# One encoder step on one core: the last down pair's second half behind the first, values and turned v in the large products' banks, gates' rows later, GpSimd's shares back on VectorE

## The chip, the cores and the metric

One core of one Trainium2 chip runs the whole kernel. Its engines are TensorE (PE, with its weight loads shown as PEld), VectorE (DVE), ScalarE (ACT), GpSimd (POOL) and SyncE (SP, which starts transfers). The metric is the time of one execution in microseconds (us), as the median of several; the profile comes from one execution of its own.

## The reference

One step of a hybrid streaming encoder layer for 512 prompt frames of a new stream and 64 frames of a running one, width 1024, feed-forward width 2816:

```python
h = layer_norm(ALPHA * x + 0.5 * swiglu_ffn(x, p['ffn1_w_gu'], p['ffn1_w_down']), p['ln1_g'], p['ln1_b'])
mix, new_state = token_mixer(h, p, conv_prev, ml_state, att_past)
h = layer_norm(ALPHA * h + mix, p['ln2_g'], p['ln2_b'])
h = layer_norm(ALPHA * h + 0.5 * swiglu_ffn(h, p['ffn2_w_gu'], p['ffn2_w_down']), p['ln3_g'], p['ln3_b'])
```

`token_mixer` multiplies `h` by one wide matrix `w_in` (mLSTM q, k, v, o, i, f; attention q, k, v; two gates), runs a chunked mLSTM with 4 heads and a band attention with 16 heads, projects both, gates them and multiplies by `w_out`. The states of the mLSTM, of its convolution and the new keys and values are outputs too.

## The kernel before, in words

**Data.** All 576 frames (512 + 64) lie along the free axis, the features in tiles of 128 partitions. A product is taken in three passes with operands split into a high part and a low part (`wh`, `wl` for weights): `wh` times high, `wh` times low, `wl` times high. Each stage works on two halves of the frames (256 + 320, or 288 + 288), so a row of 128x256, 128x288 or 128x320 in the profile is one pass over one 128-row block and one half. Almost all matmuls go through the helpers `mm` (L135) and `transpose` (L145); ScalarE's through `act` (L149), VectorE's and GpSimd's through `tt` (L152), `stt` (L155) and `ts` (L159).

**Weights.** SyncE loads a raw tile (`wr`), ScalarE casts it to `wh`, and the low part is made in one of three ways, by tables at the top: by VectorE in one operation; by VectorE in two halves of 512 columns (`PIECES`); or, for the chunks of `w_in` in `ADDED`, by a ScalarE copy of `-wh` and a GpSimd transfer that adds the raw tile in memory (`add_lo`). `("in", 48)`, `("in", 40)` and `("in", 32)` are the first three chunks of `w_in` that are used: v, k and q of the first attention head pair.

**PSUM.** There are eight banks, four with the tag "aux" (the default of `bank()`) and four with "mm" (large products). A bank is handed out again when everything that reads it is done.

**Order.** TensorE's instructions stand as the program writes them: a small event queue (`Order`) counts TensorE's time in nanoseconds as it writes matmuls, `later(dt, fn)` puts a piece of work `dt` behind, and `tick()` between matmuls lets due pieces in, along with background generators (`od.bg`: a gap and a generator). The other engines' instructions are put in order by the build's scheduler, which `high_priority` and `issue_after` steer.

**Stages that the change touches, by time in the profile.**
- *Last down pair of the first feed-forward (about 360 to 400).* The down product is taken in pairs of output tiles with seven products (`seven`, a Strassen-like scheme) into the banks X and Z (mm) and Y; `ln.take` lets VectorE add a bank to the residual tile `s`. For the last pair (6, 7) some parts are plain products (`plain`). The layer norm's first half can begin when the parts that go to half A are taken: `ln.last` sums squares, then `stats` (1-column matmuls `aux<-onec,s` and a mean), `centre` (eight `s<-s,c`, of which the tiles listed in `CP` go to GpSimd), `spread` and `apply`, and low parts `s<-s,s`. The first product of `w_in` (chunks 48, 40, 32 side by side) follows, and inside it the second half's statistics.
- *Attention (about 580 to 780).* For each pair of heads three large products give v, k and q (two passes of 256 and 320 frames each, into mm banks). q is evicted to `qs` by ScalarE and VectorE, two operations each a pass. `v_tr` turns v on TensorE into an aux bank; scores, softmax, turned probabilities (`pth`, `ptl`; `psh`, `psl` for the 64 sampled frames) and `values` and `values_s` follow from the event queue, in aux banks.
- *Attention's output projection (about 776 to 830).* `os_split` prepares sums of the heads' outputs (`Combos`) for another seven-product scheme: `Combos.begin` gives two of the four sums of tile `i + 1` to GpSimd, `Combos.add` the others to VectorE, `halves` casts the sums into `tx`.
- *mLSTM (about 840 to 1000).* v is turned by `turn5` into aux banks, with `vh` and `vl` read from them.
- *Gates' rows (around 455).* A background generator `gate_rows` takes the logarithms and cumulated sums of i and f on VectorE.
- *Second layer norm (about 1150), and the third in the tail (`turned`),* where one of four output blocks is scaled by ScalarE and GpSimd and three by VectorE.

Of the kernel before, what the change touches and what calls it, by code (L numbers as in the profile page):

```python
# [88 lines left out]
def tile_layer(ctx: ExitStack, tc: tile.TileContext, ins, outs):  # L89
# [87 lines left out]
    PIECES = {("in", 32)}  # L177

    ADDED = {("in", 48), ("in", 40)} | {("in", c + j) for c in (32, 40, 48) for j in range(2, KT)} | {("in", c) for c in (*range(2, 8), *range(10, 32), *range(56, 72))} \
# [6 lines left out]
    CP = (4, 5, 6, 7)  # L186
# [311 lines left out]
    class Norm:  # L498
# [168 lines left out]
        def turned(self, hf, dh, sq):  # L667
# [21 lines left out]
            own = nb - 1, 0  # L689
            for q in range(2):  # L690
                for b in range(nb):
                    z[b, q] = slot(F32)[:, :512]
                    if (b, q) != own:
                        last = stt(z[b, q], pts[b, q], m[:, b:b + 1], self.gb[q], ALU.subtract, ALU.mult)
                    else:
                        with tc.issue_after(last.ins):
                            last = stt(m[:, nb:nb + 1], m[:, b:b + 1], -1.0, rs[:, b:b + 1], ALU.mult, ALU.mult)
                        t = z[own]
                        act(t, pts[own], AF.Identity, scale=rs[:, b:b + 1], bias=m[:, nb:nb + 1])
                        tt(t, t, self.gb[0], ALU.mult, POOL)  # L700
                        tt(t, t, self.gb[2], ALU.add, POOL)
                        SP.dma_start(outs["yt"][b, :, 0:512], t)
            with tc.issue_after(last.ins):
                for (b, q), t in z.items():
                    if (b, q) != own:
                        stt(t, t, rs[:, b:b + 1], self.gb[2 + q], ALU.mult, ALU.add)
                        SP.dma_start(outs["yt"][b, :, q * 512:(q + 1) * 512], t)
# [56 lines left out]
    class Combos:  # L764
# [11 lines left out]
        def begin(self, i):  # L776
            r1, r2 = self.raw[4 + i], self.raw[i]
            a, b = slice(0, HT_), slice(HT_, T)
            u = self.sums[2 * i]
            tt(u[:, a], r1[:, a], r1[:, b], ALU.subtract, POOL)  # L780
            tt(u[:, b], r2[:, b], r1[:, b], ALU.subtract, POOL)

        def add(self, i, begun=False):
# [3 lines left out]
            if not begun:  # L787
                tt(u[:, a], r1[:, a], r1[:, b], ALU.subtract)
            stt(v[:, a], u[:, a], -1.0, r2[:, b], ALU.mult, ALU.subtract)
            if not begun:  # L790
                tt(u[:, b], r2[:, b], r1[:, b], ALU.subtract)
# [319 lines left out]
    def seven(n, j, inner, ln, Y=None):  # L1111
# [40 lines left out]
    def ffn(xs, n, gi, raw, final=None, prev=None):  # L1152
        hh = {}
        with tc.tile_pool(name=nm("hr"), bufs=FT, side="right", reuse_waits="tile") as hr, \
# [82 lines left out]
            with tc.tile_pool(name=nm("h1"), bufs=n1, side="right", reuse_waits="tile") as h1, \  # L1237
# [60 lines left out]
                if n == 1:  # L1298
# [133 lines left out]
    def att_qkv(j):  # L1432
# [119 lines left out]
    def att_core(j, st):  # L1552
# [51 lines left out]
        def values(e):  # L1604
            th, tl = PT[e]
            valued[0] += 1
            po = bank()
# [31 lines left out]
        def values_s(th, tl):  # L1639
            po = bank()  # L1640
# [76 lines left out]
    with tc.tile_pool(name="cx", bufs=1, side="right", reuse_waits="tile") as cx:  # L1717
# [29 lines left out]
        od.bg.append((GR, gate_rows()))  # L1747
# [20 lines left out]
    for j in range(6):  # L1768
# [3 lines left out]
        if j == 3:  # L1772
# [20 lines left out]
            def os_split():  # L1793
# [126 lines left out]
    def turn5(src, sink):  # L1920
# [392 lines left out]
```

## Time and profile before

| | |
|---|---|
| Median of 3 runs | 1563.18 us (1562.06 to 1565.11) |
| The profiled execution | 1561.61 us, its span 1559.9 us |
| TensorE busy | 1535.5 us (98% of the span) |
| VectorE, ScalarE, GpSimd busy | 73%, 57%, 16% |
| TensorE's mean granted clock | 0.995 |

A row of the profile's timeline reads: start, duration, engine, line of the kernel, operation, output tile <- inputs (numbers left out), shape, count, and in brackets the idle time before it and what ended that. A row of waits reads: engine, waiting tile and line, what it waited for, then us in total, number of times, longest. Matmuls are pipelined, so neighbouring ones overlap in the records; their pace is read from their starts.

### The profile page before, as it was taken

Reading aid. Unit: us, or ns where it says so; the run is one execution under the profiler, and the core shown is the slowest. Engines: PE = TensorE matmul, PEld = TensorE weight load, DVE = VectorE, ACT = ScalarE, POOL = GpSimd, SP = SyncE. Lnnn points to the kernel's source line nnn. Section 1 sums busy time; section 2 is a strip of 40 time slices with the busy share of each in tenths; the row PEclk is TensorE's granted clock in tenths of the full one; section 3 lists DMA queues with packets and bytes.
Section 4 is the critical chain, followed back from the end, with each engine's and each line's share of the span. In section 5 each row is a group of like instructions: output and inputs, shape, how many; then the busy total and the mean of one; then the engine's idle time right before and its main releaser. Section 6 shows DMA issues by size and latency. Waiting matters only on the chain.

```text
span 1559.9 us, 29496 instructions
## 1 busy us (share of the span) xinstructions
PE 1535.5 (98%) x11579; PEld 1520.6 (97%) x11579; DVE 1140.2 (73%) x2090; ACT 893.8 (57%) x1683; POOL 246.9 (16%) x451
## 2 busy tenths in 40 slices
PE   9999999999899999999999999999999999999997
PEld 9999999999899999999999999999999999999997
DVE  7877778676788766777586766755676877788755
ACT  7544457334665557777754877753466454557333
POOL 1000001001310015555311212202131000001002
PEclk9999999999899999999999999999999999999999
DMA  9232324534764348686534765642665222226344
GB/s 260 107 109 82 109 82 102 143 100 122 192 159 165 131 134 219 165 209 168 121 136 140 190 145 133 162 148 82 196 151 129 109 82 108 82 74 143 118 117 144
DMA packets 80836, 213.11 MB, mean 137 GB/s; under 512 B 9145, under 2 KB 21049, under 8 KB 80697
## 3 DMA queue, kind: packets, MB, share of 16 engines
q1 hardware_dynamic: 65432, 170.07, 33.1%
q0 software_dynamic: 12096, 35.33, 13.0%
q10 hardware_dynamic: 3168, 5.83, 1.1%
q8 instruction: 91, 1.49, 0.4%
q14 instruction: 49, 0.39, 0.1%
HBM read 174.23 MB, written 21.63 MB: 126 GB/s over the span
## 4 chain that ended last, share of the span: by engine, by line
PE 83%; DVE 6%; ACT 5%; DMA 2%; issue 2%; POOL 2%; DVEq 0%; SPq 0%; POOLq 0%; ACTq 0%
PE mm L135 67%; PE aux L135 14%; PE aux L145 2%; DVE wl L152 1%; DVE s L152 1%; ACT s L149 1%; ACT wh L149 1%; DMA wl<-in_w_in 1%; DMA w<-in_w_gu 1%; ACT sc L149 1%; POOL kh L159 0%; DMA wr<-in_w_dn 0%; DVE s L155 0%; ACT wh L868 0%; DVE sc L1572 0%
## 5 line engine op out<-in xcount | busy, mean ns | idle before, releaser
L135 PE MATMUL mm<-s,wh 128*128 128x288 f32 (+2 forms) x3667 | 753.6, 298 | 1.9 <-DVE st L155 0.9
L135 PEld LDWEIGHTS mm<-s,wh 128*128 128x128 f32 x3667 | 589.9, 189 | 5.7 <-DVE st L155 1.5
L135 PE MATMUL mm<-s,wl 128*128 128x288 f32 (+2 forms) x1806 | 534.5, 296 | 5.6 <-DMA wl<-in_w_in 5.6
L135 PEld LDWEIGHTS mm<-s,wl 128*128 128x128 f32 x1806 | 341.2, 189 | 6.0 <-DMA wl<-in_w_in 6.0
L149 ACT ACTIVATE wh<-wr 128x1024 fp32r<-128x1024 f32 (+2 forms) x133 | 134.2, 1016 | 148.0 <-PE mm L135 86.9
L152 DVE TENSOR_TENSOR wl<-wr,wh 128x1024 fp32r<-128x1024 f32 (+2 forms) x91 | 108.4, 1200 | 52.5 <-ACT wh L149 51.5
L135 PE MATMUL mm<-tx,wh 128*128 128x288 f32 x677 | 140.4, 296 | 0.8 <-DVE tx L152 0.8
L135 PEld LDWEIGHTS mm<-tx,wh 128*128 128x128 f32 x677 | 109.2, 188 | 1.2 <-DVE tx L152 1.0
L152 DVE TENSOR_TENSOR wl<-wt,wh 128x1024 fp32r<-128x1024 f32 x51 | 63.6, 1248 | 55.5 <-ACT wh L868 55.5
L135 PE MATMUL mm<-tx,wl 128*128 128x288 f32 x350 | 103.2, 295 | 0.0
L868 ACT ACTIVATE wh<-wt 128x1024 fp32r<-128x1024 f32 x51 | 54.0, 1059 | 84.2 <-DVE wt L152 84.2
L152 DVE TENSOR_TENSOR wl<-wu,wh 128x1024 fp32r<-128x1024 f32 x63 | 77.1, 1223 | 31.3 <-ACT wh L868 31.3
L868 ACT ACTIVATE wh<-wu 128x1024 fp32r<-128x1024 f32 x63 | 66.7, 1058 | 40.9 <-PE mm L135 35.3
L196 POOL DMA_DIRECT2D s<-s x16 | 13.7, 859 | 469.5 <-DVE hb L152 217.7
L135 PE MATMUL mm<-tx,ah 128*128 128x288 f32 x416 | 85.5, 297 | 0.4 <-ACT c L149 0.2
L149 ACT ACTIVATE h<-h 128x288 f32<-128x288 f32 x78 | 34.0, 436 | 61.0 <-DVE h L152 60.9
L135 PEld LDWEIGHTS mm<-tx,ah 128*128 128x128 f32 x416 | 66.2, 188 | 1.2 <-ACT c L149 0.6
L135 PEld LDWEIGHTS mm<-tx,wl 128*128 128x128 f32 x350 | 65.7, 188 | 0.0
L152 DVE TENSOR_TENSOR ws<-wu 128x1024 f32<-128x1024 f32 (+1 forms) x55 | 64.7, 1176 | 0.0
L152 DVE TENSOR_TENSOR wl<-ws,wh 128x1024 fp32r<-128x1024 f32 x51 | 62.2, 1219 | 3.0 <-ACT wh L868 3.0
L135 PE MATMUL mm<-h,wh 128*128 128x288 f32 (+2 forms) x304 | 62.7, 296 | 0.1
L135 PE MATMUL mm<-tx,al 128*128 128x288 f32 x208 | 61.1, 294 | 0.0
(400 smaller groups left out, 3497.3 us busy)
## 6 DMA issues: line engine op xcount, KB each, us to landing
wu<-in_w_gu SPq DMA_DIRECT2D x78, 512.0 KB, 4.4
wr<-in_w_in SPq DMA_DIRECT2D x48, 512.0 KB, 4.1
wr<-in_w_dn SPq DMA_DIRECT2D x38, 512.0 KB, 3.6
wl<-in_w_in POOLq DMA_DIRECT2D x38, 512.0 KB, 6.7
wu<-in_w_in SPq DMA_DIRECT2D x24, 512.0 KB, 4.6
wr<-in_w_dn SPq DMA_DIRECT2D x20, 384.0 KB, 4.0
s<-s POOLq DMA_DIRECT2D x16, 288.0 KB, 4.8
wu<-in_w_ap SPq DMA_DIRECT2D x8, 512.0 KB, 4.6
```

Source lines behind the costliest of these rows:

```text
L135: PE.matmul(out, lhsT, rhs, start=start, stop=stop, **kw)
L145: PE.transpose(out, in_, idn)
L149: return ACT.activation(out, in_, func, **kw)
L152: return (eng or DVE).tensor_tensor(out, a, b, op=op)
L196: return POOL.dma_start(lo, src, accum_op=ALU.add)
L868: self.last = ACT.activation(hi, src, AF.Copy)
```

## The change

1. `("in", 48)` and `("in", 40)` move from `ADDED` to `PIECES`: their low parts are made by VectorE in halves. In `seven` for pair (6, 7) the two Z products (`q1` with `t1`, `t1` with `b22`) move behind `q0 t3` and `a22 t4`, and the last takes and sums of the first half stand ahead of them (`first`).
2. `CP` becomes (6, 7): GpSimd centres two tiles of eight instead of four, in every layer norm.
3. `values`, `values_s`, `v_tr` (from the third head pair on) and the mLSTM's `turn5` of v take a "mm" bank.
4. `gate_rows` is handed to the background 20000 ns later.
5. `Combos.begin` goes, all four sums of a tile are VectorE's, with a priority for the third and fourth tile; and in the tail VectorE scales all four blocks.

```diff
-    PIECES = {("in", 32)}
-    ADDED = {("in", 48), ("in", 40)} | {("in", c + j) for c in (32, 40, 48) for j in range(2, KT)} | ...
+    PIECES = {("in", 48), ("in", 40), ("in", 32)}
+    ADDED = {("in", c + j) for c in (32, 40, 48) for j in range(2, KT)} | ...
-    CP = (4, 5, 6, 7)
+    CP = (6, 7)
...
-    def seven(n, j, inner, ln, Y=None):
+    def seven(n, j, inner, ln, Y=None, first=False):
         product(X, "t0", "t2", False)
         ln.take(j, B, X, ALU.add)
-        product(Z, "q1", "t1", True)
-        ln.take(j + 1, B, Z, ALU.subtract)
+        if not first:
+            product(Z, "q1", "t1", True)
+            ln.take(j + 1, B, Z, ALU.subtract)
         product(X, "q0", "t3", False, "v")
         ln.take(j + 1, B, X, ALU.subtract)
-        product(Z, "t1", "b22", False, "t")
-        product(X, "a22", "t4", False, "u")
+        if not first:
+            product(Z, "t1", "b22", False, "t")
+        product(X, "a22", "t4", False, None if first else "u")
         ln.take(j + 1, A, X, ALU.subtract)
+        if first:
+            first()
+            product(Z, "q1", "t1", True, "u")
+            ln.take(j + 1, B, Z, ALU.subtract)
+            product(Z, "t1", "b22", False, "t")
...
-                    Y, Z = seven(n, 6, inner, ln, Y)
-                    ln.take(6, A, Y, ALU.add)
-                    ln.last(6, A)
-                    ln.last(7, A)
+                    def first():
+                        ln.take(6, A, Y, ALU.add)
+                        ln.last(6, A)
+                        ln.last(7, A)
+                    _, Z = seven(n, 6, inner, ln, Y, first)
...
         def v_tr():
-                ps = bank()
+                ps = bank("mm" if j > 1 else "aux")
         def values(e):
-            po = bank()
+            po = bank("mm")
         def values_s(th, tl):
-            po = bank()
+            po = bank("mm")
...
-        od.bg.append((GR, gate_rows()))
+        later(20000, lambda: od.bg.append((GR, gate_rows())))
...
                 for i in range(4):
-                    if i == 0:
-                        combos.sums[0] = slot(F32)
-                    if i < 3:
-                        combos.sums[2 * i + 2] = slot(F32)
-                        combos.begin(i + 1)
-                    combos.add(i, i > 0)
-                    halves(i, 1)
+                    combos.sums[2 * i] = slot(F32)
+                    with tc.high_priority(offset=60 if i > 1 else 0):
+                        combos.add(i)
+                        halves(i, 1)
                     yield None
-                    halves(i, 0)
+                    with tc.high_priority(offset=60 if i > 1 else 0):
+                        halves(i, 0)
                     yield None
...
-                    turn5(vf, sink)
+                    turn5(vf, sink, "mm")
```

**TensorE at the last down pair.** Before; X is `mm_607`, Z is `mm_608`, and each group is twelve matmuls, of which the first and last are shown. `wh_604` with `s_456` is `q1 t1`, `wh_609` is `q0 t3`, `wh_601` with `h_503` is `t1 b22`, `wh_604` with `s_454` is `a22 t4`.

```order
L135 MATMUL mm_607_4299<-s_486_3286,wl_602_4245 128x288
L135 MATMUL mm_608_4300<-s_456_3161,wh_604_4277 128x288
...
L135 MATMUL mm_608_4300<-s_488_3291,wl_605_4278 128x288
L135 MATMUL mm_607_4299<-s_456_3161,wh_609_4304 128x288
...
L135 MATMUL mm_607_4299<-s_488_3291,wl_610_4305 128x288
L135 MATMUL mm_608_4300<-h_503_3369,wh_601_4244 128x288
...
L135 MATMUL mm_608_4300<-h_509_3417,wl_602_4245 128x288
L135 MATMUL mm_607_4299<-s_454_3156,wh_604_4277 128x288
```

And now, with the same names:

```order
L135 MATMUL mm_607_4299<-s_486_3286,wl_602_4245 128x288
L135 MATMUL mm_607_4299<-s_456_3161,wh_609_4304 128x288
...
L135 MATMUL mm_607_4299<-s_488_3291,wl_610_4305 128x288
L135 MATMUL mm_607_4299<-s_454_3156,wh_604_4277 128x288
...
L135 MATMUL mm_607_4299<-s_486_3286,wl_605_4278 128x288
L135 MATMUL mm_608_4300<-s_456_3161,wh_604_4277 128x288
...
L135 MATMUL mm_608_4300<-s_488_3291,wl_605_4278 128x288
L135 MATMUL aux_620_4404<-onec_143,s1_430_3034 128x1 x3
```

The three products of X now follow each other directly, with nothing of Z between them, and the first half's statistics come right behind `q1 t1`.

**TensorE at the sampled values of a head pair.** Now; `mm_1221` is the second pass of the query's product, `mm_1253` and `mm_1254` the turned v, `mm_1255` the sampled values.

```order
L135 MATMUL mm_1221_8123<-s_654_4589,wl_1144_7707 128x320
L145 MATMUL aux_1239_8229<-ident_133,sc_1223_8132 128x128
...
L135 MATMUL mm_1249_8252<-s_640_4510,wl_1182_7917 128x256
L145 MATMUL mm_1253_8269<-ident_133,s_1174_7904 128x128
...
L145 MATMUL mm_1254_8276<-ident_133,s_1174_7904 64x128
L135 MATMUL mm_1255_8280<-psh_1230_8181,vc_949_6712 64x64
```

Before, the last three tiles were `aux`. In the built program `mm_1255` lies in the bank of `mm_1221`, fifteen instructions behind its last matmul, and its first matmul waits for VectorE's second `qs` of `mm_1221`; the pair of heads after next has the same.

**VectorE at the attention projection's sums.** Before, from the last operation ahead of the third tile's `tx` (`tx_1580`) to the fourth's (`tx_1586`):

```order
L155 SCALAR_TENSOR_TENSOR o_1455_9369<-o_1455_9369,o_1171_7897 128x288
L152 TENSOR_TENSOR tx_1580_10029<-o_1382_8973,tx_1579_10028 128x576
L152 TENSOR_TENSOR wl_1601_10100<-wu_1540_9841,wh_1600_10099 128x1024
L152 TENSOR_TENSOR tx_1582_10033<-s_1572_9983,tx_1581_10032 128x576
L152 TENSOR_TENSOR ws_1605_10119<-wu_1541_9844 128x512
L152 TENSOR_TENSOR o_1593_10062<-mm_1595_10077,o_1593_10062 128x288
L152 TENSOR_TENSOR tx_1586_10043<-o_1455_9369,tx_1585_10042 128x576
```

And now (the third tile's `tx` is `tx_1579`; the fourth's, `tx_1586`, comes four rows behind these):

```order
L152 TENSOR_TENSOR wl_1601_10102<-wu_1540_9843,wh_1600_10101 128x1024
L152 TENSOR_TENSOR tx_1573_9988<-o_1313_8635,tx_1572_9987 128x576
L152 TENSOR_TENSOR ws_1605_10121<-wu_1541_9846 128x512
L152 TENSOR_TENSOR o_1593_10064<-mm_1595_10079,o_1593_10064 128x288
L152 TENSOR_TENSOR tx_1575_10001<-s_1571_9982,tx_1574_10000 128x576
L152 TENSOR_TENSOR wu_1541_9846<-wu_1541_9846 128x512
L152 TENSOR_TENSOR s_1584_10039<-o_1455_9371 128x288
L152 TENSOR_TENSOR s_1584_10039<-o_1171_7899,o_1455_9371 128x288
L155 SCALAR_TENSOR_TENSOR o_1455_9371<-s_1584_10039,o_1171_7899 128x288
L152 TENSOR_TENSOR tx_1579_10028<-o_1382_8975,tx_1578_10027 128x576
```

`wl_1601` stood behind the third tile's `tx` and stands ahead of it now, with the second tile's `tx`, a take and two weight steps, and the fourth tile's sums have come between.

More of the change, by code (lines that the diff above doesn't have):

```diff
@@ L176, in tile_layer @@
     NH0, NH1 = 1, 6
-    PIECES = {("in", 32)}
-    ADDED = {("in", 48), ("in", 40)} | {("in", c + j) for c in (32, 40, 48) for j in range(2, KT)} | {("in", c) for c in (*range(2, 8), *range(10, 32), *range(56, 72))} \
+    PIECES = {("in", 48), ("in", 40), ("in", 32)}
+    ADDED = {("in", c + j) for c in (32, 40, 48) for j in range(2, KT)} | {("in", c) for c in (*range(2, 8), *range(10, 32), *range(56, 72))} \
         | {("gu2", 1, 1), ("gu2", 2, 0), ("gu2", 2, 1)}
@@ L688, in turned @@
             z = {}
-            own = nb - 1, 0
             for q in range(2):
@@ L692, in turned @@
                     z[b, q] = slot(F32)[:, :512]
[L693 to L702, printed above, removed]
+                    last = stt(z[b, q], pts[b, q], m[:, b:b + 1], self.gb[q], ALU.subtract, ALU.mult)
             with tc.issue_after(last.ins):
                 for (b, q), t in z.items():
-                    if (b, q) != own:
-                        stt(t, t, rs[:, b:b + 1], self.gb[2 + q], ALU.mult, ALU.add)
-                        SP.dma_start(outs["yt"][b, :, q * 512:(q + 1) * 512], t)
+                    stt(t, t, rs[:, b:b + 1], self.gb[2 + q], ALU.mult, ALU.add)
+                    SP.dma_start(outs["yt"][b, :, q * 512:(q + 1) * 512], t)
         def centre(self, hf, bc, power):
@@ L774, in tile, with add @@
             return slot(F32R, self.pool, "tx", bufs=self.nx) if self.n <= self.nx else slot(F32R)
[L776 to L783, printed above, removed]
+        def add(self, i):
             r1, r2 = self.raw[4 + i], self.raw[i]
@@ L1918, in conv_rest, with turn5 @@
         return q, hi, lo
-    def turn5(src, sink):
+    def turn5(src, sink, tag="aux"):
         for b0, nb in ((0, 4), (4, 1)):
             w = P if b0 < 4 else NS
-            ps = bank()
+            ps = bank(tag)
             for b in range(nb):
```

6 lines of the change are left out of this document (2 added, 4 removed).

## Prediction

> **What bounds the kernel now.** I read the page first, its busy times, then TensorE's own waits, then the timeline of each place that the diff touches.
>
> ```profile
> PE 1535.5 (98%) x11579; PEld 1520.6 (97%) x11579; DVE 1140.2 (73%) x2090; ACT 893.8 (57%) x1683; POOL 246.9 (16%) x451
> PE mm L135 <- DMA wl<-in_w_in: 5.6, 2, 3.3
> PE aux L145 <- DVE ptl L152: 0.8, 1, 0.8
> PE mm L135 <- DVE st L155: 0.9, 1, 0.9
> ```
>
> TensorE (PE) is busy for 98% of the span, so only its waits can be won: 24 us of 1559.9, of which the largest group is 5.6 us for two weight transfers. The change adds and removes no matmul; it can gain what these waits (and one stretch of slow clock) cost, and it can make new ones.
>
> **Part 1: the boundary of the first layer norm (the last down pair).**
>
> ```profile
> 372.56 0.42 PE L135 MATMUL mm<-s,wh 128*128 128x288 f32 x2
> 373.20 1.23 DVE L152 TENSOR_TENSOR wl<-wr,wh 128x1024 fp32r<-128x1024 f32 x1 [1.29 <-ACT wh L149]
> 374.34 0.45 DVE L152 TENSOR_TENSOR s<-s,mm 128x288 f32<-128x288 f32 x1
> 374.94 0.50 PE L135 MATMUL mm<-s,wh 128*128 128x288 f32 x2 [0.63 <-DVE s L152]
> 376.81 0.45 DVE L152 TENSOR_TENSOR s<-s,mm 128x288 f32<-128x288 f32 x1 [1.29 <-PE mm L135]
> 381.59 0.80 PE L135 MATMUL aux<-onec,s 128*128 128x1 f32 x6
> 383.41 0.51 PE L135 MATMUL mm<-hb,wh 128*128 128x288 f32 x2
> 396.21 0.39 PE L135 MATMUL mm<-s,wl 128*128 128x256 f32 x1 [2.25 <-DMA wl<-in_w_in]
> 400.19 0.58 PE L135 MATMUL mm<-s,wl 128*128 128x256 f32 x1 [3.35 <-DMA wl<-in_w_in]
> 405.86 0.77 PE L135 MATMUL mm<-s,wh 128*128 128x256 f32 x2
> 384.00:393.00 9.00, 9.00 (x68) 8.89 (x67) 6.57 (x16) 7.88 (x15) 6.06 (x8) 1.00 0.68 170
> 397.00:398.00 1.00, 0.00 (x0) 0.00 (x0) 0.77 (x3) 0.04 (x1) 0.00 (x0) 1.00 1.07 279
> 399.00:400.00 1.00, 0.00 (x0) 0.00 (x0) 0.00 (x0) 0.00 (x0) 0.00 (x0) 0.50 0.95 332
> 405.00:408.00 3.00, 3.00 (x15) 3.00 (x16) 1.58 (x4) 1.81 (x6) 1.51 (x2) 0.50 0.06 25
> 409.05:410.85 1.80, 1.80 (x17) 1.80 (x16) 1.80 (x3) 1.43 (x3) 1.80 (x3) 1.00 0.00 0
> ```
>
> The two waits at 396.21 and 400.19 are for the low parts of two weight tiles that GpSimd adds by DMA. The last five lines are windows (their length, then busy times of PE, its weight loads, VectorE, ScalarE and GpSimd with counts, then granted clock, DMA share, GB/s): during the second wait the clock falls to half, and it stays there until past 408.
>
> Now the new order. At full clock a matmul of 288 columns takes 0.133 us (68 in the 9.00 us of 384 to 393) and one of 256 columns 0.12 (17 touch the 1.80 us of 409.05 to 410.85, two of them begun before). The twelve products of q1 with t1 that begin at 372.56 move behind the statistics of the first half. The next group now needs its bank at 372.56, and VectorE (DVE) takes it at 374.34 + 0.45, since its 1.23 us `wl` stands ahead: the wait grows from 0.63 to 2.4 us. Twelve products end at 376.5; the next take (376.81 + 0.45) makes PE wait again, to 377.3. Then twelve products (378.9), twelve more (380.5), the statistics (381.59 to 383.41 is 1.8 now; to 382.3), 54 products and the spread (389.8), 42 products (395.4), 15 of 256 columns (397.2), the second statistics (1.8; 399.0). With 0.5 us for low parts and sums that DVE delivers just in time I come to 399.5, against 405.86: **6.4 us**. Twelve matmuls behind it ran at half clock, 0.2 us each (15 in 3.00 us), and run at 0.12: 1 more. The four low parts by DVE (some 0.65 us a half, as half of the 1.23 us `wl`) and two more centring operations a half (0.45 each) come in stretches where DVE is busy for 6.57 of 9.00 us (384 to 393); ScalarE loses two casts. From 417 on, the other engines set the pace (two windows and one row):
>
> ```profile
> 417.00:437.00 20.00, 20.00 (x143) 19.84 (x143) 13.50 (x29) 19.79 (x40) 6.77 (x8) 1.00 0.97 219
> 437.00:481.00 44.00, 42.81 (x318) 42.09 (x317) 43.49 (x60) 26.20 (x41) 2.29 (x5) 1.00 0.49 142
> 407.38 2.08 DVE L152 TENSOR_TENSOR s<-s,c 128x288 f32<-128x288 f32 x2
> ```
>
> ScalarE is busy for 19.8 of 20 us, then DVE for 43.5 of 44, so PE keeps only what these two gain. They follow the second statistics, and of DVE's chain behind it the slow centring (407.38: 1.04 us each beside GpSimd, against 0.45) gets shorter. I book **-7.0 us**, from -8.3 (all of it) to -3.5 (DVE delivers late at the second statistics).
>
> At the clock I weigh a rule. The rows: the wait of 2.25 us at 396.21 left the clock at 1.00 (397 to 398), and 3.35 us more, after one short burst, brought 0.50. The Trainium skill ("TensorE: Matmul & The Clock Gate", Part 1) says that the clock falls to half after a whole idle window of some 3.4 us, which runs freely. By that rule alone the new 2.4 us wait keeps the full clock and part 1 stays at -7.0; the burst before the fall here was short, so the rows alone leave a smaller wait possible, and I keep the fall as a rival.
>
> **Part 2: values, sampled values and the turned v in the "mm" banks.** This frees "aux" banks, but a mm bank comes free only when the large product that it held has been read.
>
> ```profile
> 679.37 0.27 PE L135 MATMUL aux<-psh,vc 128*64 128x64 f32 x1
> 678.85 1.05 ACT L149 ACTIVATE wh<-wr 128x1024 fp32r<-128x1024 f32 x1
> 681.02 0.43 ACT L149 ACTIVATE qs<-mm 64x320 fp32r<-64x320 f32 x1
> 681.48 0.49 DVE L155 SCALAR_TENSOR_TENSOR qs<-mm,qs 64x320 fp32r<-64x320 f32 x1 [1.42 <-ACT qs L149]
> 634.12 0.19 PE L135 MATMUL aux<-psh,vc 128*64 128x64 f32 x1
> 634.23 0.68 DVE L152 TENSOR_TENSOR o<-aux,tmp 64x512 f32<-64x512 f32 x1
> 963.90 0.40 PE L135 MATMUL mm<-s,wh 128*128 128x256 f32 x2
> 963.89 0.88 DVE L152 TENSOR_TENSOR vl<-aux,vh 128x512 fp32r<-128x512 f32 x2
> 988.73 0.28 PE L135 MATMUL aux<-vh,W 128*128 128x258 f32 x1
> 989.07 0.37 ACT L149 ACTIVATE hf<-aux 128x258 f32<-128x258 f32 x1
> ```
>
> In the changed program the sampled values of two head pairs get the bank of the query's second pass, and their first matmul waits for DVE's last `qs` of it. At the first place that matmul starts at 679.37 now, and the `qs` ends at 681.48 + 0.49, because ScalarE's share of the work (681.02) stands behind two casts of 1.05 us, the first at 678.85. That order doesn't change, so TensorE will wait about 2.6 us there, and as long two head pairs later, where the same instructions follow each other: 5.2. At 634.12 the same matmul gets the bank of the values that DVE reads until 634.92: 0.8 us more, in spite of the 0.8 us wait on `ptl` (in the list above) that goes just before it. In the mLSTM a product that starts at 963.90 gets the bank of a turned v, whose reader is the first of the two `vl` from 963.89 (about 0.7 of their 0.88 us), and a state product at 988.73 a bank that ScalarE reads until 989.07 + 0.37: 0.7 each. Small waits that go, and later ones that shrink because the other engines have caught up, give back 1.2, an estimate. Sum: **+6.2**, from +3.5 (half of the first two places) to +7.5.
>
> **Part 3: the attention projection's sums.**
>
> ```profile
> 797.34 1.06 DVE L155 SCALAR_TENSOR_TENSOR o<-s,o 128x288 f32<-128x288 f32 x1
> 800.06 1.05 ACT L868 ACTIVATE wh<-wu 128x1024 fp32r<-128x1024 f32 x1
> 804.75 0.45 DVE L152 TENSOR_TENSOR o<-mm,o 128x288 f32<-128x288 f32 x1
> 805.12 0.75 DVE L152 TENSOR_TENSOR tx<-o,tx 128x576 fp32r<-128x576 f32 x1
> 805.78 0.69 DVE L152 TENSOR_TENSOR wu<-wu 128x512 f32<-128x512 f32 x1
> 805.92 0.40 PE L135 MATMUL mm<-tx,wh 128*128 128x288 f32 x1 [0.80 <-DVE tx L152]
> ```
>
> Six GpSimd operations go to DVE, where one of 288 columns takes 0.37 us (804.75 to 805.12): 2.2 us more on an engine that PE already waits for at 805.92. GpSimd's shadow goes with them (1.06 against 0.45 at 797.34, and about as much at two more operations), some 1.8. But DVE's order changes too: the third and fourth `tx` now stand behind a `wl`, a take and steps on the weights. That `wl` waits for the cast at 800.06 + 1.05, which I let begin a microsecond earlier, since the `tx` cast ahead of it on ScalarE moves behind it. Walking DVE from 800 (1.2 for `wl`, 0.66 for a `tx`, 0.37 for a sum, 0.63 for a weight step) the third `tx` ends at 806.0 and the fourth at 808.4, so PE's 805.92 becomes 808.4: **+2.5**, from +1.2 to +3.6.
>
> **Part 4: GpSimd's shares at the second layer norm and in the tail; the gates' rows.**
>
> ```profile
> 1164.52 0.39 PE L135 MATMUL mm<-s,eh 128*128 128x256 f32 x1 [0.76 <-DVE s L152]
> 1551.76 3.79 DVE L155 SCALAR_TENSOR_TENSOR s<-s,rs,s 128x512 f32<-128x512 f32 x3
> ```
>
> With two GpSimd operations instead of four, DVE's low parts run undisturbed there, and the wait of 0.76 us and a smaller one ahead of it go: **-1.0** (0 to -1.1). In the tail three operations take 3.79 us beside GpSimd, and undisturbed ones would need some 0.7 each, 1.7 less; against that stand one more operation on DVE in this row and one ahead of it: **-0.6** (0 to -0.9). The gates' rows: DVE's operations for them stand in the same places as before, and only five TensorE transposes move, so the 0.9 us wait on `st` (in the list above) stays: **0** (-0.9 if it goes).
>
> **Sum.** -7.0 + 6.2 + 2.5 - 1.0 - 0.6 = +0.1. The profiled execution took 1561.61 us (span 1559.9 and 1.7 around it), which becomes 1561.7; the median of the runs shown is 1.57 above the profiled one, so I forecast **1563.3 us**: the gain at the first layer norm is spent on bank waits and sums.
>
> **The rivals.** About 0.2% (3.1 us) is what a measurement of this kernel can tell from no change.
> - *Slower, the clock falls.* The wait of 2.4 us at 372.6 and the next of 0.8 us lie within 5 us; if the gate counts them as idle, PE runs at half clock until it has been busy for a while, as from 400.2 to past 408: some 8.4 us at half, so 4.2 us lost, 1567.5. It decides as soon as the clock in 375 to 385 reads under 1.00. For it: the fall at 398 to 399 came after 1.5 to 2 us of an unbroken wait. Against: 2.25 us did nothing. 10%.
> - *Slower, VectorE late at the second statistics.* The low parts and centring operations queue ahead of the last sums, and part 1 brings 3.5: 1566.8. 12%.
> - *Faster, the boundary pays more.* The gates' rows or the shorter centring relieve DVE in 437 to 481, so the wait on `st` goes (0.9), part 1 gives 8.3 and the sums cost 1.2: 1563.3 - 0.9 - 1.3 - 1.3 = 1559.8. 22%.
> - *Faster, the bank waits don't come* (another bank, or `qs` sooner than now): without the 5.2 us 1558.1. Against it stands the fixed order on ScalarE. 8%.
>
> **How the numbers follow.** My forecast has 48%. The two faster cases make 30% for faster by over 0.2%, the two slower ones 22%; 48% within. The range reaches past the cases on both sides by the unknowns of parts 2 and 3: 1557 to 1568. Forecast alone: 1560 to 1566.
>
> **What would show it.** Right: no wait on `wl<-in_w_in` and clock 1.00 in 395 to 410; a wait of about 2.4 us on `s` near 375; two waits of about 2.6 us on `qs` in the attention stage, which nothing there has now; a `tx` wait near 800 of 2 to 3 us instead of 0.8; the tail half a microsecond shorter. Wrong: no `qs` waits, a half clock near 375, or the second statistics later than 401.

## The result, and the profile after

The changed kernel takes **1568.19 us** (median of 14 runs, 1566.21 to 1573.5) against 1562.43 us (14 runs) for the kernel before on the same chips: a ratio of **1.0046, 95% interval 1.0035 to 1.0056**. It is slower by about 0.5%, where 1563.3 and no change had been forecast, and the end of the range (1568.0) is just missed. The profiled execution took 1567.9 us, its span 1566.2: 6.3 more than the profiled execution before.

Three views of the changed kernel. Its busy times, then TensorE's waits (us in total, times, longest), first lines of the list:

```profile
PE 1536.7 (98%) x11579; PEld 1522.5 (97%) x11579; DVE 1143.5 (73%) x2111; ACT 893.1 (57%) x1682; POOL 228.7 (15%) x431
```

```profile
PE mm L135 <- DVE qs L155: 5.0, 2, 2.5
PE mm L135 <- DVE s L152: 2.8, 3, 2.1
PE mm L135 <- DVE tx L152: 2.1, 2, 1.3
PE mm L145 <- DVE qs L155: 1.8, 1, 1.8
PE mm L135 <- ACT vf L149: 1.8, 1, 1.8
...
PE mm L135 <- DVE st L155: 0.9, 1, 0.9
```

The 5.6 us for the two weight transfers are gone, as predicted. In their place stand the waits that the prediction named, at nearly its sizes (two on `qs` of 2.5, one on `s` of 2.1, `tx` of 1.3 and less), the unmoved 0.9 on `st`, and two that it did not have: 1.8 us on `vf`, and 1.8 on `qs` at a turned v (L145). The timeline shows where they are; of a row with a count, the time is that of its first instruction:

```profile
375.43 0.52 PE L135 MATMUL mm<-s,wh 128*128 128x288 f32 x2 [2.09 <-DVE s L152]
414.01 0.56 PE L135 MATMUL mm<-s,wh 128*128 128x320 f32 x2 [1.84 <-ACT vf L149]
680.27 0.22 PE L135 MATMUL mm<-psh,vc 128*64 128x64 f32 x1 [2.50 <-DVE qs L155]
728.87 0.22 PE L135 MATMUL mm<-psh,vc 128*64 128x64 f32 x1 [2.50 <-DVE qs L155]
810.80 0.40 PE L135 MATMUL mm<-tx,wh 128*128 128x288 f32 x1 [1.27 <-DVE tx L152]
813.11 0.61 PE L135 MATMUL mm<-tx,wh 128*128 128x288 f32 x1 [0.83 <-DVE tx L152]
```

The waits alone do not make the time. The windows below (length, busy times of PE, its weight loads, DVE, ScalarE, GpSimd with counts, granted clock, DMA share, GB/s) are cut, but for 395 to 410, on the grid of 3.41 us on which the trace's record of the clock changes. They show, for four of these places, the 3.41 us that hold the wait, or most of it, and the time behind:

```profile
372.40:375.81 3.41, 1.32 (x11) 1.12 (x10) 2.06 (x4) 1.39 (x2) 0.00 (x0) 1.00 0.29 96
375.81:382.64 6.83, 6.28 (x26) 5.94 (x26) 1.87 (x3) 0.84 (x1) 0.00 (x0) 0.50 0.46 134
395.00:410.00 15.00, 15.00 (x119) 14.63 (x119) 13.88 (x32) 9.54 (x24) 7.44 (x9) 1.00 0.72 259
676.18:679.59 3.41, 1.59 (x14) 1.32 (x12) 1.92 (x4) 3.35 (x6) 3.00 (x6) 1.00 0.84 201
679.59:683.00 3.41, 2.73 (x32) 2.76 (x33) 1.73 (x4) 1.79 (x6) 2.83 (x8) 1.00 0.62 168
727.38:730.79 3.41, 1.92 (x26) 1.95 (x27) 1.38 (x3) 2.17 (x7) 2.07 (x6) 1.00 0.78 211
730.79:734.20 3.41, 3.41 (x18) 3.41 (x17) 0.94 (x3) 0.79 (x2) 2.26 (x6) 0.50 0.56 91
809.30:812.71 3.41, 1.17 (x5) 0.48 (x4) 3.41 (x8) 1.59 (x3) 0.00 (x0) 1.00 0.28 113
812.71:816.12 3.41, 3.01 (x12) 3.01 (x13) 2.35 (x4) 1.53 (x3) 0.00 (x0) 0.50 0.49 118
```

Behind three of the new waits TensorE runs at **half clock**, for 6.83, 3.41 and 3.41 us; behind the one at 680 it does not. In 395 to 410, where the clock was at half before, it is 1.00 now. Following each matmul through both traces (the start of the same instruction after, less its start before) gives where the 6.3 us come from: +0.6 by 36 us (in the traces of this study that stretch is 0.0 to 2.1 us longer than in the kernel before's), -3.3 over the first layer norm, +7.5 at the bank waits, +1.3 for the half clock at 731, +2.1 at the `tx` waits, +1.3 for the half clock at 813, -1.0 at the second layer norm and -1.5 in the tail: +7.0, of which steps of 0.3 us and less in between take back 0.7.

The runs differ more than before, and with their clock: the eight with a mean granted clock of 0.993 to 0.995 took 1566.2 to 1568.4 us, the six with 0.990 to 0.992 took 1570.4 to 1573.5.

### The profile page after: what moved, and what is told of

It reads as the page before. It is cut to its first block, busy times and chain, and to the rows that moved or that the text cites. A ratio compares the mean times of both kernels' runs of the same rounds, so it can differ in the third digit from the quotient of the medians.

```text
span 1566.2 us, 29485 instructions
## 1 busy us (share of the span) xinstructions
PE 1536.7 (98%) x11579; PEld 1522.5 (97%) x11579; DVE 1143.5 (73%) x2111; ACT 893.1 (57%) x1682; POOL 228.7 (15%) x431
## 3 DMA queue, kind: packets, MB, share of 16 engines
q8 instruction: 91, 1.49, 0.4%
## 4 chain that ended last, share of the span: by engine, by line
PE 89%; DVE 4%; ACT 4%; POOL 1%; issue 1%; DMA 0%; ACTq 0%; DVEq 0%; POOLq 0%; SPq 0%
PE mm L135 74%; PE aux L135 13%; PE aux L145 1%; DVE wl L152 1%; DVE s L152 1%; ACT wh L149 1%; ACT sc L149 1%; POOL kh L159 1%; DMA wr<-in_w_dn 0%; ACT L149 0%; DVE s L155 0%; DVE sc L1562 0%; ACT s L149 0%; ACT wl L149 0%; PE mm L145 0%
```

## The experiments

Theory: each wait costs its length, and besides, it may halve the clock: the granted clock is set once in every 3.41 us, on a grid that runs freely, and falls when TensorE was idle for too much of one such stretch. So the same wait halves the clock in one execution and not in the next. Rival: the parts cost their waits, as predicted, and the excess is in the parts themselves. Times are medians; the kernel before had 1562.3 to 1562.4 in all three groups of runs.

**e1, the boundary alone.** `PIECES`, `ADDED`, `seven` and the last pair as changed:

```diff
-    PIECES = {("in", 32)}
+    PIECES = {("in", 48), ("in", 40), ("in", 32)}
...
+                    _, Z = seven(n, 6, inner, ln, Y, first)
```

> The kernel before with the first part alone (last down pair's second-half products behind the first half's, low parts of the two weight tiles by VectorE). Theory: the wait of 2.2 us that this order puts near 373 leaves TensorE less than about half busy over one 3.4 us stretch, so the granted clock falls to half for 3.4 to 6.8 us around 376 to 383 in this profile and in most runs, and a new wait of about 1.8 us on vf near 412 takes back what TensorE has won over ScalarE: about 3 us below the kernel before (1559.5), with runs of lower mean clock longer. Rival (the step as predicted): the clock stays at 1.00 there and all of 7 us is kept: 1555.5.

Measured: **1557.86**, ratio 0.9967 (0.9955 to 0.9979). The six runs: 1554.92, 1554.99 and 1556.8 with clocks of 0.998, 0.999 and 0.997; 1558.92, 1560.25 and 1560.83 with 0.994, 0.995 and 0.994. The profiled one is of the first kind. Its windows, on the grid that its own last fall (in the tail) fixes, and the wait on `vf`:

```profile
370.69:374.10 3.41, 2.31 (x17) 2.02 (x16) 2.18 (x4) 1.39 (x2) 0.00 (x0) 1.00 0.65 202
374.10:377.51 3.41, 2.05 (x13) 1.84 (x14) 1.49 (x4) 0.80 (x1) 0.00 (x0) 1.00 0.52 154
377.51:384.00 6.49, 6.49 (x50) 6.38 (x50) 5.04 (x10) 2.02 (x5) 0.81 (x1) 1.00 0.22 64
```

```profile
374.92 0.51 PE L135 MATMUL mm<-s,wh 128*128 128x288 f32 x2 [1.91 <-DVE s L152]
410.48 0.56 PE L135 MATMUL mm<-s,wh 128*128 128x320 f32 x2 [0.65 <-ACT vf L149]
```

The same wait is there, but a border of the grid cuts it: 1.10 us of idle time in one stretch and 1.36 in the next (which also holds a second, short wait), and the clock stays at 1.00. So both expectations were half right: the boundary is worth the predicted 7 us in the two shortest runs (1562.4 - 1555.0 = 7.4), and 1.6 to 3.5 in the three with the lower clock. Where the clock fell in those three no trace shows: their means stand for some 11 to 14 us more at half speed than the profiled run has, about twice the 6.83 us of the fall at 375.81, so another place must have had its share. A fall seems to cost more than its own half speed: here the wait on `vf` ends at 410.48, in the changed kernel, with the fall, at 414.01. That ScalarE's and VectorE's chain behind the second statistics comes later with TensorE is argued from this, and the two kernels differ in the centring too.

**e2, the banks alone.**

```diff
-            po = bank()
+            po = bank("mm")
...
-                    turn5(vf, sink)
+                    turn5(vf, sink, "mm")
```

> The kernel before with the values, the sampled values and the turned v in the large products' banks, and nothing else. Theory: waits of 2.6 us near 679 and near 725 on qs, 0.8 near 634, 0.6 near 964, sum 6.4; besides, each of the two large ones can halve the clock for 3.4 us, depending on where the stretches of 3.4 us begin in that run, so single runs differ by 1.1 to 1.7 us a fall: +7 in the median (1569.5), runs between 1568 and 1573, those with the lower mean clock the longer. Rival: the waits alone, 6.2 in every run (1568.6), with mean clock and spread as in the kernel before.

Measured: **1571.96** (1571.13 to 1576.74), ratio 1.0066 (1.0054 to 1.0078). Mean clocks 0.992 in the three shorter runs, 0.990 in the two longer. In the profiled run (1575.12) all three waits halve the clock, the first for 6.83 us; the other two:

```profile
683.78:687.19 3.41, 0.90 (x13) 0.67 (x11) 1.83 (x4) 3.01 (x5) 2.80 (x6) 1.00 0.97 280
687.19:690.60 3.41, 3.41 (x25) 3.41 (x24) 0.93 (x3) 1.03 (x3) 2.80 (x8) 0.50 0.47 97
734.98:738.39 3.41, 1.44 (x22) 1.48 (x23) 1.38 (x3) 2.22 (x5) 2.75 (x7) 1.00 0.65 196
738.39:741.80 3.41, 3.41 (x19) 3.41 (x18) 0.69 (x1) 0.83 (x3) 1.94 (x6) 0.50 0.74 126
```

Instruction by instruction against the kernel before, this execution loses 1.0 at 633 (a turned v that waits 1.86 for `qs`, less the 0.8 on `ptl` that goes), 2.7 at 679, 2.7 at 725 and 0.8 at 964: 7.2 of waits; and 2.9 + 1.5 + 1.4 = 5.8 behind the first three at half clock. Together 13.0; its time is 12.7 above the median before. The theory's mechanism holds, but its sizes were short, by 2.5 in the median, and two of the five runs lie above its 1573: it had not counted on a fall at 633.

**e3, the sums alone** (`Combos.begin` goes, all four sums by VectorE, with the priority):

```diff
-            if not begun:
-                tt(u[:, a], r1[:, a], r1[:, b], ALU.subtract)
+            tt(u[:, a], r1[:, a], r1[:, b], ALU.subtract)
...
+                    with tc.high_priority(offset=60 if i > 1 else 0):
+                        combos.add(i)
```

> The kernel before with the attention projection's sums by VectorE alone (no beginning by GpSimd), and nothing else. Theory: three tx waits near 804 to 809 (1.4, 0.7 and 1.1 us in the changed kernel's profile) cost 2.5 us, and a fall of the clock behind them, when it comes, 1.3 to 1.7 more: +2.5 to +4.2, median 1565.7. Rival: the VectorE time of the six operations (2.2 us) lies beside other work and nothing is lost in this kernel, where TensorE comes to the place earlier or later than in the changed one: 1562.5.

Measured: **1566.09**, ratio 1.0021 (1.0013 to 1.003). The waits are those of the changed kernel:

```profile
807.75 0.40 PE L135 MATMUL mm<-tx,wh 128*128 128x288 f32 x1 [1.27 <-DVE tx L152]
808.83 0.40 PE L135 MATMUL mm<-tx,wh 128*128 128x288 f32 x1 [0.56 <-ACT tx L149]
810.05 0.40 PE L135 MATMUL mm<-tx,wh 128*128 128x288 f32 x1 [0.83 <-DVE tx L152]
```

Matmul by matmul the stage loses 2.1 here, and in this execution the clock did not fall behind the waits. That is less than the 3.7 of the medians. Another 1.7 of this execution was there by 36 us, where the change does nothing; in the other runs the rest has no place that a trace shows. Their mean clocks, 0.992 to 0.994 against 0.993 to 0.996 before, leave room for a fall in some of them.

**e4, two centring operations and the tail alone.**

```diff
-    CP = (4, 5, 6, 7)
+    CP = (6, 7)
...
-            own = nb - 1, 0
```

In the tail everything goes that treats the block `own` apart (ScalarE's and GpSimd's share).

> The kernel before with two of the four centring operations taken from GpSimd and the tail's share of GpSimd and ScalarE taken back, and nothing else. Theory: 0.8 at the second layer norm and about 1.5 in the tail: 1560.1. The prediction's own terms were 1.0 and 0.6 (1560.8). Rival: the tail after is shorter only by where its last DMA happened to land in one profile, and the centring at the first layer norm costs VectorE what it saves at the second: 1562.4.

Measured: **1559.8**, ratio 0.9984 (0.9975 to 0.9992), as the theory had it: 1.0 at the second layer norm, and 1.5 between the last `var` and the end.

**e5, the boundary with the wait filled.** As e1, and in the wait 14 matmuls into the bank W, which the program overwrites later:

```diff
+        if idle is not None:
+            wh = parts[ids["t"]][0]
+            for i in range(14):
+                PE.matmul(idle, wh[:, 0:P], inner.b[0]["t2"][0], start=True, stop=False, skip_group_check=True)
```

> The boundary alone (as e1_boundary) with 14 matmuls of 288 columns more, 1.9 us, put into the wait of 2.2 us near 373; they go into a bank that the program overwrites later, and compute nothing that is used. Theory: idle time is what halves the clock there, so busy work in the same time keeps it at 1.00: every run at a mean clock of 0.997 or more and at 1555 (1554 to 1556.5), where e1_boundary without them had three runs at 1555 to 1557 and three at 1559 to 1561 with a clock of 0.994 to 0.995. Rival: the spread of e1_boundary has another cause (a DMA that lands late, say): the same two groups and a median of 1557.9, or up to 1.9 longer, for the added work.

Measured: **1556.33**, ratio 0.9959 (0.9947 to 0.9972); the five runs, in order of time from 1554.73 to 1558.32, with clocks of 0.999, 0.999, 0.997, 0.998, 0.998. The added work takes up the wait, and no run has the 0.994 to 0.995 that three of e1's six had. What is left below 1.00 in the profiled run is a fall at another place:

```profile
372.50:377.00 4.50, 4.41 (x32) 3.97 (x30) 2.00 (x4) 1.27 (x3) 0.00 (x0) 1.00 0.47 148
397.54:400.95 3.41, 2.54 (x20) 2.23 (x19) 2.34 (x6) 1.70 (x5) 0.82 (x3) 1.00 0.89 267
400.95:404.36 3.41, 3.41 (x19) 3.41 (x18) 2.92 (x9) 2.33 (x7) 3.22 (x3) 0.50 0.95 359
```

The median lies 1.5 below e1's, with intervals that overlap. With the same order of the products but TensorE busy, the clock near 376 holds here; it held in e1's profiled run too, and none of five runs against three of six is little to go by. So e5 fits idle time as the cause, and e9 shows it.

**e6, the q1 products left in their place**, only `t1` with `b22` behind the first half (a variant of e1):

```diff
-        if not first:
-            product(Z, "q1", "t1", True)
-            ln.take(j + 1, B, Z, ALU.subtract)
+        product(Z, "q1", "t1", True)
+        ln.take(j + 1, B, Z, ALU.subtract)
```

> The boundary alone, but with the products of q1 with t1 left in their old place between those of t0 with t2 and of q0 with t3; only t1 with b22 still stands behind the first half's statistics. Theory: the waits of 2.2 and 0.8 us on s near 374 and 378 shrink to 0.6 and less, the clock has nothing to fall for, and what TensorE wins above e1_boundary's undisturbed runs it gives back on vf near 412, since ScalarE sets the pace there: 1554.5 (1553 to 1556) in every run. Rival: the first half's statistics, 1.6 us later, hold up the chain of VectorE and ScalarE behind them, so the whole boundary is later: 1557 or more.

Measured: **1556.21** (1554.48 to 1557.36), ratio 0.9957 (0.9943 to 0.997), clocks 0.996 to 0.999. The long wait is gone, but in the profiled run the clock falls at the second statistics instead (396 to 410 at 0.76), behind a stretch with only 1.25 us of idle time, so the theory was too sure of "every run", and the median lies just above its 1553 to 1556:

```profile
395.16:398.57 3.41, 2.16 (x16) 1.90 (x16) 3.41 (x9) 1.90 (x4) 1.83 (x4) 1.00 0.95 326
396.00:410.00 14.00, 12.75 (x78) 12.40 (x77) 10.57 (x26) 7.76 (x20) 7.47 (x8) 0.76 0.48 172
```

**e7, the changed kernel without the sampled values' bank.** In `values_s`:

```diff
-            po = bank("mm")
+            po = bank()
```

> The changed kernel with only the sampled values put back into the small results' banks. Theory: the two waits of 2.6 us on qs near 679 and 725 go, and with them the falls of the clock behind them (one of 1.1 us in the changed kernel's profile, up to two in other runs): 5.2 + 1.1 to 2.4 less than the changed kernel's 1568.2, 1561.5 (1560.5 to 1563). Rival: only the waits, 1563.0, or other waits that stood behind them come instead: above 1564.

Measured: **1561.44**, ratio to the kernel before 0.9996 (0.9987 to 1.0005). That one line is worth 6.75 us against the changed kernel's median. Its two waits are 5.4 of that by the starts; that the other 1.35 is half clock behind them fits the theory, and is what is left, not measured apart.

**e8, what pays, together**: e6's order with e4's edits, against the kernel before:

```diff
-    PIECES = {("in", 32)}
+    PIECES = {("in", 48), ("in", 40), ("in", 32)}
...
-    CP = (4, 5, 6, 7)
+    CP = (6, 7)
...
+        if first:
+            first()
+            product(Z, "t1", "b22", False, "t")
```

> The parts that pay, together: the boundary of e6_between, two centring operations instead of four on GpSimd, and the tail's share taken back; banks, sums and gates' rows as in the kernel before. Theory: they lie at different places and add up: 7.5 + 2.6 below the kernel before's 1562.4, so 1552.5 (1551 to 1554) in every run. Rival: the two centring operations that come to VectorE at the first layer norm take up its time behind the boundary (two more in each half, 0.45 us each) and cost 1 to 2 of it: 1554 to 1555.

Measured: **1550.37** (1550.16 to 1551.04), ratio **0.9922 (0.991 to 0.9935)**: it beats both kernels. Clocks 0.998 to 0.999 in each run. Its busy times, and two windows around the boundary:

```profile
PE 1531.5 (99%) x11579; PEld 1517.4 (98%) x11579; DVE 1142.6 (74%) x2105; ACT 891.6 (58%) x1682; POOL 236.7 (15%) x437
```

```profile
370.00:384.00 14.00, 12.93 (x94) 11.95 (x93) 9.77 (x20) 4.84 (x8) 0.13 (x1) 1.00 0.50 160
395.00:410.00 15.00, 14.32 (x113) 13.75 (x112) 13.44 (x35) 12.11 (x30) 9.44 (x9) 1.00 0.68 224
```

The gain is 12.0, two more than the 10.1 expected and 3.2 more than e6 and e4 measured (6.1 and 2.6): with two centring operations on GpSimd the clock stays at 1.00 at the second statistics, where e6 lost it. Why VectorE comes in time there was not tried by itself.

**e9, the clock by itself:** one stream of 288-column matmuls, broken 107 times by a chain of VectorE operations. This kernel leaves the whole layer out and writes zeros.

```diff
+            for i in range(n):
+                PE.matmul(ps[:, :N], w, rhs if i or carry is None else carry, start=i == 0, stop=i == n - 1)
...
+            for i in range(k):
+                DVE.scalar_tensor_tensor(out=s, in0=ps[:, :N], scalar=1e-4, in1=raw[:, :N], op0=ALU.mult, op1=ALU.mult)
```

> Not the layer: the outputs are zeros. A stream of TensorE matmuls of 288 columns, 48 to 73 without a break, broken 107 times by a wait for 1 to 9 VectorE operations of 0.45 us (waits of about 0.7 to 4.5 us, 12 of most lengths, at changing places of the 3.41 us grid). It measures after which waits the granted clock falls. Theory: it falls when TensorE was idle for about two thirds (2.2 us) of one stretch of the grid, so never after waits below 2 us, after some of those of 2.4 to 3.4 us (those that lie within one stretch: 5 to 35%), after half or more from 4 us. The rule by which a whole stretch must be idle: no fall at all below 3.4 us and few of the longest.

Measured, from the trace's record of the clock (all its changes lie a whole number of 3.413 us apart):

| Wait of TensorE, us | 0.5 | 1.0 | 1.5 | 2.0 | 2.5 | 3.0 | 3.5 | 4.0 | 4.5 |
|---|---|---|---|---|---|---|---|---|---|
| waits | 12 | 12 | 12 | 12 | 12 | 12 | 12 | 11 | 12 |
| clock fell | 0 | 0 | 0 | 9 | 11 | 10 | 11 | 11 | 12 |

What decides is the idle time within one stretch of the grid: of the 107 waits, every one with at least 1.85 us of it in one stretch halved the clock, and none with 1.77 or less. A wait of 3.0 us that a border cuts in two does nothing; one of 2.0 us inside a stretch does (two timelines and the windows behind them):

```profile
810.47 0.40 PE L123 MATMUL mm<-s,x 128*128 128x288 f32 x1 [3.01 <-DVE s L126]
```

```profile
805.75:809.16 3.41, 1.72 (x14) 1.48 (x12) 1.55 (x4) 0.00 (x0) 0.00 (x0) 1.00 0.00 0
809.16:812.58 3.42, 2.11 (x16) 2.11 (x17) 1.19 (x3) 0.00 (x0) 0.00 (x0) 1.00 0.00 0
812.58:816.00 3.42, 3.42 (x29) 3.42 (x28) 0.00 (x0) 0.00 (x0) 0.00 (x0) 1.00 0.00 0
```

```profile
180.56 0.40 PE L123 MATMUL mm<-s,x 128*128 128x288 f32 x1 [2.03 <-DVE s L126]
```

```profile
177.70:181.11 3.41, 1.38 (x11) 1.15 (x10) 1.83 (x4) 0.00 (x0) 0.00 (x0) 1.00 0.00 0
181.11:184.53 3.42, 3.42 (x16) 3.42 (x16) 0.00 (x0) 0.00 (x0) 0.00 (x0) 0.50 0.00 0
```

My limit of 2.2 us had been too high, and the chances with it too low.

**e10, e8 with the change's own order of the q1 products:**

```diff
-        product(Z, "q1", "t1", True)
-        ln.take(j + 1, B, Z, ALU.subtract)
+        if not first:
+            product(Z, "q1", "t1", True)
+            ln.take(j + 1, B, Z, ALU.subtract)
```

> The boundary as in the changed kernel, with its two centring operations and its tail; banks, sums and gates' rows as before (e8_best with the changed kernel's own order of the products of q1 with t1). Theory: the wait of 2.2 us near 373 is back, and with it the fall of the clock in a share of the runs: some at 1550 to 1552 with a clock of 0.998, some 3 to 4 longer at 0.994 to 0.996, median 1553. Rival: the order makes no difference here, 1550.4 with a clock of 0.998 or more in each run.

Measured: **1556.27**, ratio 0.9954 (0.9941 to 0.9966): 1553.06 and 1553.5 at a clock of 0.998, and 1556.27, 1557.03 and 1557.38 at 0.995 to 0.997. The profiled run is of the second kind, with the wait inside one stretch:

```profile
373.06:376.47 3.41, 1.55 (x12) 1.34 (x11) 1.96 (x3) 0.91 (x2) 0.00 (x0) 1.00 0.37 111
376.47:383.30 6.83, 6.28 (x27) 5.94 (x27) 2.78 (x5) 1.29 (x2) 0.00 (x0) 0.50 0.37 121
```

Moving the q1 products behind the first half costs 5.9 us against e8; some 3 of it also where the clock holds, which the theory did not have: its median was 1553. Inside this kernel the profiled run, with the fall, lies 2.8 to 3.2 above the two runs at 0.998.

**e11, the sums without the priority** (from e3):

```diff
-                    with tc.high_priority(offset=60 if i > 1 else 0):
-                        combos.add(i)
-                        halves(i, 1)
+                    combos.add(i)
+                    halves(i, 1)
```

> The sums by VectorE alone as in e3_sums, without the priority that the change gives to the third and fourth of them (VectorE and ScalarE then take a few operations there in another order). Theory: VectorE's 2.2 us more and the weight steps between them set the loss, 1566.0 as in e3_sums or up to 1 more. Rival: the priority's order is what costs, and without it TensorE waits as in the kernel before: 1562.4 to 1563.5.

Measured: **1564.86**, ratio 1.0018 (1.0009 to 1.0026), against e3's 1.0021 (1.0013 to 1.003). The intervals overlap, and in the two profiled executions the stage loses the same, 2.1 in e3 and 2.2 here, with the waits at other places (2.09 and 0.88 here). So the loss is the sums' on VectorE, and these traces give the priority no cost; the 1.2 between the medians has no place in them.

**e12, the gates' rows alone.**

```diff
-        od.bg.append((GR, gate_rows()))
+        later(20000, lambda: od.bg.append((GR, gate_rows())))
```

> The kernel before with the gates' rows alone begun later. Theory: nothing, as the parts' sum leaves (boundary -4.6, banks +9.5, sums +3.7, centring and tail -2.6 make +6.0 against +5.8 for all): 1562.4 within 0.7. Rival: the wait of 0.9 us on st near 453 goes: 1561.5, or VectorE's work for the rows falls upon a place where TensorE waits for it: 1563.5.

Measured: **1562.56**, ratio 0.9999 (0.999 to 1.0008): nothing. The parts by themselves add up: -4.55 (e1), +9.55 (e2), +3.68 (e3), -2.61 (e4), +0.17 (e12) make +6.2, and the whole change has +5.8. As each median holds falls that come by chance, that they agree so well is in part luck.

## Why the prediction was wrong, point by point

**The step that failed is the clock's.** Part 1 let the rule decide by which "the new 2.4 us wait keeps the full clock", gave the fall a chance of 10%, and parts 2 and 3 did not weigh the clock at all, not even for two waits of 2.6 us. By e9's limit a wait stays harmless only when a border of the grid leaves less than 1.85 us of it on either side: for the 2.1 us near 375 in (3.70 - 2.1) / 3.41 = 47% of the cases, for each 2.5 us at 680 and 729 in 35%. So a fall was the likelier outcome at each of the three places. At the first the traces show it in the changed kernel, in e7 and in e10, and not in e1, where a border cuts the wait; three of e1's six runs and three of e10's five have the lower clocks. In the changed kernel's profile the falls behind the waits cost 1.3 and 1.3 at 731 and 813, and some 3.0 to 3.4 at the boundary (3.0 within e10's runs; -3.3 here against -6.65 in e1's profile, with the clock at 1.00). Without these 5.6 to 6.0 us its 6.3 would be 0.3 to 0.7, near the +0.1 of the sum. That it is so near is in part luck: the bank waits were 1.3 larger than booked, the tail and small steps made up for it.

**How the trace misled.** I read two things in it: 2.25 us at 396.21 left the clock alone, and the fall came "after 1.5 to 2 us of an unbroken wait". Cut on the grid, the same trace says another thing:

```profile
391.83:395.25 3.42, 2.13 (x17) 1.93 (x15) 3.35 (x8) 3.42 (x10) 1.86 (x4) 1.00 1.02 244
395.25:398.66 3.41, 0.63 (x3) 0.42 (x3) 2.52 (x6) 1.36 (x3) 0.74 (x3) 1.00 1.06 276
398.66:402.00 3.34, 1.81 (x8) 1.81 (x9) 0.00 (x0) 0.00 (x0) 0.00 (x0) 0.50 1.03 385
```

A border at 395.25 split the 2.25 us into 1.28 and 0.96, and the second stretch held 0.96 + 1.83 = 2.8 us of idle time: the first wait had its share in the fall. The Trainium skill ("TensorE: Matmul & The Clock Gate", Part 1) says that the window runs freely, and the traces agree (in the changed kernel the falls at 375.81, 730.79 and 812.71 lie 104 and 24 times 3.413 us apart). It also gives a whole idle window as what brings the clock down; the runs differ, and they decide: 1.85 us of 3.41 were enough.

**Part 1, -7.0.** The walk was right: a wait of 2.4 near 375 (2.09 in its row, 2.25 by the starts), the matmuls behind the second statistics 5.9 us earlier in e1's profile (6.4), -6.65 behind them, -7.4 in e1's two shortest runs. That PE keeps only what the other engines gain was said; it showed as the wait on `vf`.

**Part 2, +6.2.** The two waits of 2.6 came as walked (2.7 each by the starts, in the changed kernel and in e2). At 633 not the values but a turned v waits, for `qs`: +1.0 for 0.8. At 964 +0.8 for 0.7; at 988.7 +0.3 for 0.7. Of the 1.2 "given back" at most 0.7 came. The rest is the clock, in the traces; of e2's median, 9.55, that is argued.

**Part 3, +2.5.** Waits of 1.27, 0.55 and 0.83, where 0.80 had been, lose 2.1, near the predicted size; the clock adds 1.3 in the changed kernel's execution. **Part 4:** -1.0 for -1.0 at the second layer norm, 0 for 0 at the gates' rows; in the tail -1.5 for -0.6, because VectorE's chain shrinks by 0.6 as walked (four operations now take 2.73 us, three took 3.79).

```profile
1560.03 2.73 DVE L155 SCALAR_TENSOR_TENSOR s<-s,rs,s 128x512 f32<-128x512 f32 x4
```

The end of the span, behind the last output transfer, comes 0.9 sooner still.

**The rivals.** "The clock falls" was the right mechanism at the right place with the right mark (a clock under 1.00 in 375 to 385), and 1567.5 is close; its price there (4.2) was near the 3.0 to 3.4 found. It lacked the two other places and, above all, chance. The other slower rival (VectorE late at the second statistics) did not come in the changed kernel: the clock in 395 to 410 is 1.00 and TensorE has no wait there. It did come in e6, with four centring operations on GpSimd: a wait of 1.25 us on `s`, and a fall. Neither faster rival came.

## What to carry to other kernels

When a change makes a TensorE wait of about 2 us or more, price it at its length plus a share of a halved clock: find the grid from the trace's record of the clock, count idle time per stretch, and for a new wait take the chance that it falls inside one. Prefer two short waits that lie apart to one long, or keep products to put between; and before giving a tile a bank, ask whose last reader frees it, since one such line cost 6.75 us here. A change of many parts deserves a run of each: the parts that paid were worth 12.0 us together, with e6's order of the products, and were hidden behind the two that did not.

## What the runs showed of the hardware

- The granted clock changes only at steps of 3.413 us, at a phase that differs from execution to execution (a border at 374.10 in e1, at 375.81 in the changed kernel); it fell after at least 1.85 us of idle time in one stretch and never after 1.77 or less (107 waits in e9), and stayed at half for one to four stretches (3.41 to 13.65 us).
- The same limit holds in the layer. In the traces of both kernels and of the eleven runs of the layer, 18 stretches between 30 us and the tail have a fall behind them; 15 of them held at least 1.85 us of idle time, and no stretch with that much kept the clock. Two stretches of e7, with 1.848 and 1.850 us, lie on either side:

```profile
628.71:632.12 3.41, 1.56 (x14) 1.35 (x13) 2.56 (x7) 3.25 (x8) 2.94 (x7) 1.00 0.42 110
410.26:413.67 3.41, 1.56 (x14) 1.36 (x12) 2.47 (x6) 3.41 (x9) 0.52 (x1) 1.00 0.51 154
```

- The second of them holds the wait on `vf`, 1.85 us long, and the clock fell behind it; waits of 1.84 and 1.89 us at the same place in the changed kernel and in e10 were cut by a border, and it did not.
- In the other three of the 18, stretches with many small matmuls, less idle time was enough: 1.49 us in the changed kernel's 727.38 to 730.79 (18 of its 26 matmuls have 64 columns), 1.25 in e6's 395.16 to 398.57 (six one-column matmuls) and 0.87 in e5's 397.54 to 400.95 (twelve). That such matmuls count for less than their time is argued from these three rows, not tried.
- Work that nobody needs filled a wait at no cost in time: e5, with 14 matmuls more in a wait of 2 us, lies 1.5 us below e1 in the median (the intervals overlap), and none of its five runs has a mean clock under 0.997, where three of e1's six have 0.994 to 0.995.
